# Rotary embedding on half the head: from sixteen 2 MB tiles to four 8 MB tiles, with tables broadcast over heads

## Chip, core and metric

The kernel runs on one core of a Trainium2 chip. The metric is the time of one execution on the device in microseconds (us), the median of several runs. Traces come from one profiled execution.

## What is computed

x has the shape (16, 512, 16, 64): batch, sequence, heads, dim, in fp32. That is 33.55 MB, read once and written once. Of each head's 64 numbers the first 32 are rotated in pairs (element j with element j+16), by a cosine and a sine that depend on the sequence position and on j; the last 32 pass unchanged. Only the first 16 columns of the tables cos and sin, each (512, 32), are used.

```python
x1, x2 = x[..., :32], x[..., 32:]
first  = x1[..., :16] * cos[..., :16] - x1[..., 16:] * sin[..., :16]
second = x1[..., :16] * sin[..., :16] + x1[..., 16:] * cos[..., :16]
return concatenate([first, second, x2], axis=-1)
```

## The kernel before

One tile is one batch element: 512 sequence rows of 1024 numbers, four rows on each of 128 partitions. A tile is 2 MB, and each partition holds one contiguous run of 16 KB of HBM. There are 16 tiles, six buffers for x (pool xp), and four for the products a_t and b_t (pool abp).

The tables come first. POOL issues the loads of cos and sin into cosL and sinL (L39, L40), on the software queue q0. POOL then spreads them over the heads and over the two halves of a rotated block, into CCX and SSX, one copy for each of the four rows (L49, L50). So CCX and SSX have an element for every element that VectorE multiplies.

Then a loop runs over the 16 tiles. SP issues the load of x_t (L57). VectorE (DVE in the profile) multiplies the first half of each head by the cosines into a_t (L64) and by the sines into b_t (L65), and writes differences and sums of quarters back into x_t (L66, L72). ACT issues the store of the whole tile, with the untouched half in it (L79). The in-place result means that an x buffer is free only when its store has landed; SP's seventh load waits for the first store. Loads run on the queue q1 or q10, stores on the other; both feed the same 16 DMA engines. The order within each engine's instructions is set by the framework's scheduler from the dependences, and semaphores connect the engines.

Of the kernel before, what the change touches and what calls it, by code (L numbers as in the profile page):

```python
# [1 line left out]

# [4 lines left out]


@with_exitstack  # L10
def kernel(
    ctx: ExitStack,
    tc: tile.TileContext,
    x: bass.AP,
    cos: bass.AP,
    sin: bass.AP,
    out: bass.AP,
):
    nc = tc.nc
    fp32 = mybir.dt.float32  # L20

    B, S, H, D = x.shape
    Q = D // 4
    HF = D // 2
    P = 128
    K = S // P

    xf = x.rearrange("b (p k) h d -> b p (k h d)", p=P)
    of = out.rearrange("b (p k) h d -> b p (k h d)", p=P)
    cosf = cos.rearrange("(p k) j -> p (k j)", p=P)  # L30
    sinf = sin.rearrange("(p k) j -> p (k j)", p=P)

    const_pool = ctx.enter_context(tc.tile_pool(name="const", bufs=1))
    x_pool = ctx.enter_context(tc.tile_pool(name="xp", bufs=6))
    ab_pool = ctx.enter_context(tc.tile_pool(name="abp", bufs=4))

    cosL = const_pool.tile([P, K, HF], fp32)
    sinL = const_pool.tile([P, K, HF], fp32)
    nc.gpsimd.dma_start(out=cosL[:], in_=cosf)  # L39
    nc.gpsimd.dma_start(out=sinL[:], in_=sinf)  # L40

    CCX = const_pool.tile([P, K, H, 2, Q], fp32)
    SSX = const_pool.tile([P, K, H, 2, Q], fp32)
    for k in range(K):
        dst_c = CCX[:, k].rearrange("p h c j -> p (h c) j")
        dst_s = SSX[:, k].rearrange("p h c j -> p (h c) j")
        src_c = cosL[:, k : k + 1, 0:Q].to_broadcast((P, 2 * H, Q))
        src_s = sinL[:, k : k + 1, 0:Q].to_broadcast((P, 2 * H, Q))
        nc.gpsimd.tensor_copy(out=dst_c, in_=src_c)  # L49
        nc.gpsimd.tensor_copy(out=dst_s, in_=src_s)  # L50

    cc_op = CCX.rearrange("p k h c j -> p (k h) (c j)")
    ss_op = SSX.rearrange("p k h c j -> p (k h) (c j)")

    for b in range(B):
        x_t = x_pool.tile([P, K, H, D], fp32)
        nc.sync.dma_start(out=x_t.rearrange("p k h d -> p (k h d)"), in_=xf[b])  # L57

        a_t = ab_pool.tile([P, K * H, HF], fp32)
        b_t = ab_pool.tile([P, K * H, HF], fp32)  # L60

        x12 = x_t.rearrange("p k h d -> p (k h) d")[:, :, 0:HF]

        nc.vector.tensor_mul(out=a_t[:], in0=x12, in1=cc_op)  # L64
        nc.vector.tensor_mul(out=b_t[:], in0=x12, in1=ss_op)  # L65
        nc.vector.tensor_tensor(  # L66
            out=x12[:, :, 0:Q],
            in0=a_t[:, :, 0:Q],
            in1=b_t[:, :, Q : 2 * Q],
            op=mybir.AluOpType.subtract,  # L70
        )
        nc.vector.tensor_tensor(  # L72
            out=x12[:, :, Q : 2 * Q],
            in0=a_t[:, :, Q : 2 * Q],
            in1=b_t[:, :, 0:Q],
            op=mybir.AluOpType.add,
        )

        nc.scalar.dma_start(out=of[b], in_=x_t.rearrange("p k h d -> p (k h d)"))  # L79


# [1 line left out]
_INS = ['x', 'cos', 'sin']  # L83
_OUTS = [((16, 512, 16, 64), 'float32')]


# [23 lines left out]
```

## Time and profile before

| | before |
|---|---|
| median of 9 runs | 163.16 us (162.98 to 163.54) |
| the profiled execution | 163.15 us |
| its span in the trace | 161.4 us |
| VectorE busy | 108.7 us |
| GpSimd (POOL) busy | 6.0 us |
| moved by DMA | 67.25 MB, mean 417 GB/s over the span |
| first store issued | 19.2 us |

The span runs from the first to the last record of the program; what the execution's time has beyond it is start and end that the trace does not show. Issuing a transfer is not counted as busy time. "DMA" in the rows by time is the mean busy share of the 16 DMA engines.

### The profile page before, as it was taken

What the parts mean: (1) busy time and instruction counts of PE and PEld (TensorE: products, weight loads), DVE (VectorE), ACT (ScalarE), POOL (GpSimd) and SP (SyncE); (2) the same over time, 40 slices, a digit from 0 to 9 for tenths busy, and PEclk for the clock granted to TensorE, in tenths of its full rate; (3) what the DMA queues carried; (4) which work ended last, traced back from release to release, by engine and by line L of the source; (5) the groups of instructions that cost most, each with busy time, mean ns of one, the idle gap of its engine ahead of it and who ended that gap; (6) DMA issues with size and microseconds to landing.
All of it is one profiled execution on the core that took longest, in us unless ns stands there. A gap on an engine that the chain in (4) does not pass through costs nothing.

```text
span 161.4 us, 189 instructions
## 1 busy us (share of the span) xinstructions
DVE 108.7 (67%) x64; POOL 6.0 (4%) x14
## 2 busy tenths in 40 slices
DVE  0009999999995692948849296592947939389300
POOL 3190000000000000000000000000000000000000
DMA  5999999999999999999999999999999999999994
GB/s 158 426 430 430 418 386 426 443 422 435 439 422 430 439 414 443 422 430 447 414 439 439 422 435 430 430 430 422 439 439 418 439 435 424 430 426 439 435 414 207
DMA packets 4673, 67.25 MB, mean 417 GB/s; under 512 B 544, under 2 KB 544, under 8 KB 576
## 3 DMA queue, kind: packets, MB, share of 16 engines
q1 hardware_dynamic: 2304, 33.56, 49.4%
q10 hardware_dynamic: 2304, 33.56, 48.6%
q0 software_dynamic: 64, 0.13, 0.2%
q14 instruction: 1, 0.01, 0.0%
HBM read 33.69 MB, written 33.55 MB: 417 GB/s over the span
## 4 chain that ended last, share of the span: by engine, by line
DMA 60%; DVE 28%; POOL 2%; issue 2%; DVEq 1%; POOLq 0%; SPq 0%; PEldq 0%
DMA out_dram<-x_t 32%; DMA x_t<-in_x_dram 24%; DVE a_t L64 9%; DVE b_t L65 8%; DVE x_t L66 6%; DVE x_t L72 5%; DMA cosL<-in_cos_dram 4%; POOL CCX L49 1%; DVEq L105 1%; POOL SSX L50 1%; POOLq L105 0%; SPq L57 0%; DVEq L66 0%; PEldq L105 0%
## 5 line engine op out<-in xcount | busy, mean ns | idle before, releaser
L64 DVE TENSOR_TENSOR a_t<-x_t,CCX 128x2048 f32<-128x2048 f32 x16 | 37.0, 2314 | 41.9 <-DMA x_t<-in_x_dram 30.0
L65 DVE TENSOR_TENSOR b_t<-x_t,SSX 128x2048 f32<-128x2048 f32 x16 | 36.6, 2285 | 0.0
L66 DVE TENSOR_TENSOR x_t<-a_t,b_t 128x1024 f32<-128x1024 f32 x16 | 19.6, 1222 | 0.2
L72 DVE TENSOR_TENSOR x_t<-a_t,b_t 128x1024 f32<-128x1024 f32 x16 | 19.5, 1219 | 0.0
L49 POOL COPY CCX<-cosL 128x512 f32<-128x512 f32 x4 | 2.4, 615 | 5.1 <-DMA cosL<-in_cos_dram 5.1
L50 POOL COPY SSX<-sinL 128x512 f32<-128x512 f32 x4 | 2.4, 616 | 0.3 <-DMA sinL<-in_sin_dram 0.3
L39 POOL DMA_DIRECT2D cosL<-in_cos_dram x1 | 0.7, 671 | 0.8 <-PEq L105 0.8
L40 POOL DMA_DIRECT2D sinL<-in_sin_dram x1 | 0.5, 537 | 0.0
L94 POOL MEMSET const-float32-0.0<- 128x1 f32 x1 | 0.1, 100 | 0.2 <-issue 0.2
L94 POOL MEMSET const-bfloat16-1.0<- 128x1 bf16 x1 | 0.1, 103 | 0.0
L94 POOL MEMSET const-uint8-127<- 128x1 uint8 x1 | 0.1, 103 | 0.0
L94 POOL MEMSET const-float32-1.0<- 128x1 f32 x1 | 0.1, 100 | 0.0
## 6 DMA issues: line engine op xcount, KB each, us to landing
x_t<-in_x_dram SPq DMA_DIRECT2D x16, 2048.0 KB, 19.4
out_dram<-x_t ACTq DMA_DIRECT2D x16, 2048.0 KB, 24.1
cosL<-in_cos_dram POOLq DMA_DIRECT2D x1, 64.0 KB, 6.3
sinL<-in_sin_dram POOLq DMA_DIRECT2D x1, 64.0 KB, 7.1
```

The lines of the kernel that those rows point to most:

```text
L39: nc.gpsimd.dma_start(out=cosL[:], in_=cosf)
L40: nc.gpsimd.dma_start(out=sinL[:], in_=sinf)
L49: nc.gpsimd.tensor_copy(out=dst_c, in_=src_c)
L50: nc.gpsimd.tensor_copy(out=dst_s, in_=src_s)
L64: nc.vector.tensor_mul(out=a_t[:], in0=x12, in1=cc_op)
L65: nc.vector.tensor_mul(out=b_t[:], in0=x12, in1=ss_op)
L66: nc.vector.tensor_tensor(out=x12[:, :, 0:Q], in0=a_t[:, :, 0:Q], in1=b_t[:, :, Q : 2 * Q], op=mybir.AluOpType.subtract,)
L72: nc.vector.tensor_tensor(out=x12[:, :, Q : 2 * Q], in0=a_t[:, :, Q : 2 * Q], in1=b_t[:, :, 0:Q], op=mybir.AluOpType.add,)
L94: nc = _bacc.Bacc("TRN2", target_bir_lowering=False, num_devices=1)
L105: with _tile.TileContext(nc) as tc:
```

## The change

The sequence rows are cut differently: 16 rows to a partition (K = 16), so a tile is four batch elements, 8 MB, and a partition holds one contiguous run of 64 KB. There are four tiles and three buffers for x. SP loads the first tile in pieces of 4, 4 and 8 rows per partition, the second and third whole, and the fourth in two halves. Three tiles are stored whole and the fourth in halves.

With 16 rows on a partition, 32 partitions hold all 512 positions, and the table repeats every 32 partitions. ACT loads cos and sin into 32 partitions (stage), and four copies, two by VectorE and two by POOL, write the used columns twice over into each group of 32 partitions of table. CCX and SSX are gone: VectorE reads the table with a step of zero over the heads.

VectorE works in chunks of four rows per partition (KC = 4), the same 128x4096 elements as a tile before. The sine products go into b_t, which now lies in PSUM, with two buffers; the cosine products are written in place into x_t, so a_t is gone.

```diff
-    K = S // P
-    x_pool = ctx.enter_context(tc.tile_pool(name="xp", bufs=6))
-    ab_pool = ctx.enter_context(tc.tile_pool(name="abp", bufs=4))
-    nc.gpsimd.dma_start(out=cosL[:], in_=cosf)
-    nc.gpsimd.dma_start(out=sinL[:], in_=sinf)
...
+    K = 16
+    T = B * S // (P * K)
+    PB = S // K
+    REP = P // PB
+    xf = x.rearrange("b s h d -> (b s h d)").rearrange("(t p f) -> t p f", t=T, p=P)
...
+    x_pool = ctx.enter_context(tc.tile_pool(name="xp", bufs=3))
+    b_pool = ctx.enter_context(tc.tile_pool(name="bp", bufs=2, space=bass.MemoryType.PSUM))
+    stage = const_pool.tile([PB, 2, K, HF], fp32)
+    nc.scalar.dma_start(out=stage[:, 0].rearrange("p k j -> p (k j)"), in_=cosf)
+    nc.scalar.dma_start(out=stage[:, 1].rearrange("p k j -> p (k j)"), in_=sinf)
+    table = const_pool.tile([P, 2, K, 2, Q], fp32)
+    for r in range(REP):
+        eng = nc.vector if r % 2 == 0 else nc.gpsimd
+        eng.tensor_copy(
+            out=table[r * PB : (r + 1) * PB].rearrange("p t k c j -> p (t k) c j"),
+            in_=stage.rearrange("p t k j -> p (t k) j")[:, :, 0:Q]
+            .unsqueeze(2)
+            .to_broadcast((PB, 2 * K, 2, Q)),
+        )
...
+    KC = 4
+    loads = [[4, 4, 8]] + [[16]] * (T - 2) + [[8, 8]]
+    stores = [[16]] * (T - 1) + [[8, 8]]
     for t in range(T):
         x_t = x_pool.tile([P, K, H, D], fp32)
+        for n in loads[t]:
+            nc.sync.dma_start(
+                out=x_f[:, k0 * R : (k0 + n) * R], in_=xf[t, :, k0 * R : (k0 + n) * R]
+            )
...
+        for k0 in range(0, K, KC):
+            x1 = x_t[:, k0 : k0 + KC, :, 0:HF]
+            c = C[:, k0 : k0 + KC].unsqueeze(2).to_broadcast((P, KC, H, HF))
+            s = Sn[:, k0 : k0 + KC].unsqueeze(2).to_broadcast((P, KC, H, HF))
+            b_t = b_pool.tile([P, KC, H, HF], fp32)
+            nc.vector.tensor_mul(out=b_t[:], in0=x1, in1=s)
+            nc.vector.tensor_mul(out=x1, in0=x1, in1=c)
+            nc.vector.tensor_sub(
+                out=x1[:, :, :, 0:Q], in0=x1[:, :, :, 0:Q], in1=b_t[:, :, :, Q:HF]
+            )
+            nc.vector.tensor_add(
+                out=x1[:, :, :, Q:HF], in0=x1[:, :, :, Q:HF], in1=b_t[:, :, :, 0:Q]
+            )
+            for lo, hi in ends:
+                if hi == k0 + KC:
+                    nc.scalar.dma_start(
+                        out=of[t, :, lo * R : hi * R], in_=x_f[:, lo * R : hi * R]
+                    )
```

In the changed kernel the table copies are L50, the loads of x L68, the four VectorE operations L81, L82, L83 and L86, and the stores L91. The scheduler keeps the order chunk by chunk for the first two chunks and then interleaves the chunks in pairs.

More of the change, by code (lines that the diff above doesn't have):

```diff
@@ L20 @@
     fp32 = mybir.dt.float32
+    P = 128
     B, S, H, D = x.shape
@@ L24 @@
     HF = D // 2
-    P = 128
-    K = S // P
[L28 to L31, printed above, removed]
-    const_pool = ctx.enter_context(tc.tile_pool(name="const", bufs=1))
-    x_pool = ctx.enter_context(tc.tile_pool(name="xp", bufs=6))
-    ab_pool = ctx.enter_context(tc.tile_pool(name="abp", bufs=4))
-    cosL = const_pool.tile([P, K, HF], fp32)
@@ L38 @@
-    sinL = const_pool.tile([P, K, HF], fp32)
-    nc.gpsimd.dma_start(out=cosL[:], in_=cosf)
-    nc.gpsimd.dma_start(out=sinL[:], in_=sinf)
[L42 to L50, printed above, removed]
@@ L52 @@
-    cc_op = CCX.rearrange("p k h c j -> p (k h) (c j)")
-    ss_op = SSX.rearrange("p k h c j -> p (k h) (c j)")
-    for b in range(B):
-        x_t = x_pool.tile([P, K, H, D], fp32)
[L57 to L79, printed above, removed]
+    K = 16
@@ new lines @@
+    T = B * S // (P * K)
+    PB = S // K
+    REP = P // PB
+    R = H * D
+    xf = x.rearrange("b s h d -> (b s h d)").rearrange("(t p f) -> t p f", t=T, p=P)
+    of = out.rearrange("b s h d -> (b s h d)").rearrange("(t p f) -> t p f", t=T, p=P)
+    cosf = cos.rearrange("(p k) j -> p (k j)", k=K)
+    sinf = sin.rearrange("(p k) j -> p (k j)", k=K)
+    const_pool = ctx.enter_context(tc.tile_pool(name="const", bufs=1))
+    x_pool = ctx.enter_context(tc.tile_pool(name="xp", bufs=3))
+    b_pool = ctx.enter_context(tc.tile_pool(name="bp", bufs=2, space=bass.MemoryType.PSUM))
@@ new lines @@
+    C = table[:, 0].rearrange("p k c j -> p k (c j)")
+    Sn = table[:, 1].rearrange("p k c j -> p k (c j)")
+    KC = 4
+    loads = [[4, 4, 8]] + [[16]] * (T - 2) + [[8, 8]]
+    stores = [[16]] * (T - 1) + [[8, 8]]
+    for t in range(T):
+        x_t = x_pool.tile([P, K, H, D], fp32)
+        x_f = x_t.rearrange("p k h d -> p (k h d)")
+        k0 = 0
+        for n in loads[t]:
+            nc.sync.dma_start(
+                out=x_f[:, k0 * R : (k0 + n) * R], in_=xf[t, :, k0 * R : (k0 + n) * R]
+            )
+            k0 += n
+        ends, k0 = [], 0
+        for n in stores[t]:
+            ends.append((k0, k0 + n))
+            k0 += n
+        for k0 in range(0, K, KC):
[16 more added lines that the diff above has]
+                    )
```

## Prediction

> **What bounds the kernel now.** I read the page's second and third parts first, because a kernel that loads everything, does four VectorE operations and stores everything can be bound by either side.
>
> ```profile
> span 161.4 us, 189 instructions
> DVE 108.7 (67%) x64; POOL 6.0 (4%) x14
> DMA  5999999999999999999999999999999999999994
> DMA packets 4673, 67.25 MB, mean 417 GB/s; under 512 B 544, under 2 KB 544, under 8 KB 576
> q1 hardware_dynamic: 2304, 33.56, 49.4%
> q10 hardware_dynamic: 2304, 33.56, 48.6%
> DMA 60%; DVE 28%; POOL 2%; issue 2%; DVEq 1%; POOLq 0%; SPq 0%; PEldq 0%
> L64 DVE TENSOR_TENSOR a_t<-x_t,CCX 128x2048 f32<-128x2048 f32 x16 | 37.0, 2314 | 41.9 <-DMA x_t<-in_x_dram 30.0
> ```
>
> The DMA row is full from the second slice to the last but one, while DVE is busy for 67%. The chain gives DVE 28%, but those steps lie where the DMA row shows a 9 as well: the chain follows one order of release and does not say that the DMA engines rested. The wait of 30.0 us at L64 is DVE waiting for data. So the question is where the 16 DMA engines do not run at full rate. Then the table by windows (columns: window, length, DVE busy, POOL busy, clock, DMA share, GB/s):
>
> ```profile
> 0.00:4.00 4.00, 0.00 (x0) 1.41 (x6) 1.00 0.56 152
> 4.00:20.00 16.00, 8.07 (x5) 4.57 (x8) 1.00 1.01 430
> 20.00:24.00 4.00, 3.96 (x3) 0.00 (x0) 1.00 0.97 369
> 24.00:158.00 134.00, 96.67 (x58) 0.00 (x0) 1.00 1.01 431
> 158.00:161.40 3.40, 0.00 (x0) 0.00 (x0) 1.00 0.36 154
> ```
>
> At 431 GB/s the 67.25 MB need 156.0 us. The first 4 us move 0.61 MB, worth 1.4 us: 2.6 lost. The window 20 to 24, where the first store (issued at 19.2) begins, loses 4 x (431-369)/431 = 0.6. The last 3.4 us move 0.52 MB: 2.2 lost, mostly after the last byte. 156.0+2.6+0.6+2.2 = 161.4, the span. The profiled execution took 163.15, so 1.75 us lie around the span; the median of the 9 runs is 163.16, the same within 0.01.
>
> [...]with equal rows q1 and q10 move 33.56 MB each, and loads (19.4 us to landing) and stores (24.1) each stay about two transfers deep at one transfer per 9.7 us. [...]The trace shows only a pitch of 16 KB, at 431/2 = 215.5 per direction. [...]no PSUM operation is in the trace.
>
> **The change part by part.**
>
> *Transfers.* 16 loads and 16 stores of 2 MB become 7 loads and 5 stores of 2, 4 or 8 MB, with the same x bytes, and two table loads stay. Rows per engine go from 256 of 16 KB to 96: loads 24+8+8+16, stores 8+8+8+16. One 16 KB row takes 16 x 16384/431000 = 0.608 us of an engine[...]. [...] I take -0.6.
>
> *Start.* SP still issues a 2 MB load first (0.75 us); the table loads move from POOL to ACT, which had nothing to issue until 19.2. Same bytes: 0, between -0.3 and +0.3. POOL loses its two issues (0.67+0.54 us), which nobody else waits behind.
>
> *Tables.* Eight POOL copies of 512 (4.8 us) become two on DVE and two on POOL of 1024 elements. With a POOL copy at 0.615 us for 512, one of 1024 is 1.2[...]. In pairs side by side 2.4 us, one after another at most 4.8. The cos load took 6.3 us to land; from ACT at about 0.8 that gives 7.1 (bounds 3 and 8), so tables are ready at about 9.5 (5 to 13). Before, DVE began at 11.9. The first 2 MB are moved by 2.6+4.9 = 7.5, seen at about 9.5. Covered entirely: the first store is later than this by four chunks and DMA has three tiles to load meanwhile.
>
> *VectorE.* Work per 128x4096 elements stays 2048+2048+1024+1024. Before, one set takes 6.80 us from start to start (19.07 to 25.87). b_t in PSUM is touched by three of four operations[...]; the extra order waits on DVE's own results cost about 0.1 us (2.32 against 2.21 us from start to start in the row of L65). A broadcast table (step 0 over heads) is not in the trace: 0 to +0.2, taken 0[...]. I take 7.05 us per chunk, 6.8 to 7.3. Hidden by the DMA if stores never run dry, which is the next step.
>
> *Order of work, at 431 and equal shares.* The load pieces of tile 0 are seen at 9.5, 14.3 and 24.1. Chunks 0 and 1 end by 23.6, chunks 2 and 3 at 38.2; store 0 (8.39 MB) moves from 39.5. Until then loads ran alone and have moved 15.9 MB. Tile 1 needs 0.9 MB more at half rate: 43.4, seen at 45.4; DVE idles 7 us, then works to 73.6, store 1 is queued by 75. Store 0 ends at 39.5+38.9 = 78.4. SP's load of tile 3 waits for it, with nothing behind it on SP but that tile's second half; tile 2's load still runs (43.4+38.9 = 82.3), so the load queue never empties. Tile 2 is computed from 84.4 to 112.6, store 2 queued at 114. Tile 3's halves arrive at 101.8 and 121.3 (+2). Store 1 ends at 117.3. Store 2 has half rate until 121.3, then all: 138.8. Last halves of the compute end at 126.7 and 140.8; their stores are queued by 128 and 142 behind store 2, and run to 148.6 and 158.3. The last one is in the queue 6.6 us before its turn. So each queue that stops leaves the other one full, and the later first store (39 against 19) costs no DMA time. If an engine serves whole rows in turn, tile 3's 32 KB rows get a third beside 64 KB stores: the second half arrives near 130, the last store is queued near 147.5, 1 us ahead of its turn. Still 0, but the cover is thin.
>
> *Store start.* The 0.6 us hole should recur near 39 us: 0, between -0.6 and +1 with longer rows. Reads alone last 20 us longer, at 430 against 431: +0.05.
>
> **Sum**: 161.4-0.6+0.05 = 160.8, plus 1.75: about 162.5 us.
>
> **Rivals.**
> 1. *The pitch in HBM slows every transfer.* Neighbouring partitions lie 64 KB apart instead of 16 in all stages. [...] Against: [...]every tile is one contiguous 8 MB. It decides from a loss of 0.2%, or 0.6% if the row saving comes in full.[...]
> 2. *Rows bring nothing*, because bytes set the 431 or because a 64 KB row is cut into packets as short as today's, so that the change is not what it says: 163.2 us. For it: the DMA share is 1.00 already.
> 3. *VectorE becomes the bound at the end.* DVE has two idle stretches (7 and 11 us) while whole 8 MB loads land. If stores take two thirds throughout and a chunk takes 7.5 us, tile 3's second half is ready some 4 us after store 2 and its first half have drained: about 166.5. Even split and 7.05 us speak against; at even shares it takes 8.5 us a chunk.
>
> **How the numbers follow.** A measurement of this kernel tells about 0.2%, 0.33 us, from no change. Longer rows at work: 0.50, all faster. Rival 2: 0.22, no change. Slower: rival 1 0.18, rival 3 and a larger hole at the store's start 0.10. [...]High end: rival 1 with its estimate, 165.3, which leaves out about one in ten above. If DMA goes as I say, 161.6 to 163.3 is its own range.
>
> **What would show it.** Right: far fewer packets on q1 and q10; a rate of 433 to 434 in the windows of both directions; a full DMA row; L81 near 2.3 us; idle of DVE before tiles 1 and 2; the last store issued near 142. Wrong: a rate under 430 in steady windows (rival 1), packets of 16 KB or a rate of 431 (rival 2), a gap in the DMA row after 120 us (rival 3), a deeper slice near 39 us.

## The result and the profile after

The changed kernel takes 181.65 us (median of 10 runs, 180.3 to 183.23) where the kernel before takes 163.17 (31 runs). The ratio is 1.1114, with a 95% interval of 1.1095 to 1.1134: 11% slower. The forecast was 162.5 us with a range of 161.0 to 165.3. The profiled execution took 183.64 us, with a span of 181.9; it is some 2 us longer than the median, so a loss read from its trace can be too large by as much.

The page after, in the lines that answer to those shown of before:

```profile
span 181.9 us, 145 instructions
DVE 109.6 (60%) x66; POOL 3.2 (2%) x6
DMA  6999979999899989798999999999999989400595
DMA packets 1825, 67.25 MB, mean 370 GB/s; under 512 B 224, under 2 KB 224, under 8 KB 288
q1 hardware_dynamic: 1008, 33.55, 46.0%
q10 hardware_dynamic: 816, 33.69, 44.5%
...
L81 DVE TENSOR_TENSOR b_t<-x_t,table 128x2048 f32<-128x2048 f32 x16 | 36.1, 2296 | 51.6 <-DMA x_t<-in_x_dram 50.6
```

Same bytes, fewer packets, nearly the same VectorE work (109.6 us, before 108.7). The DMA row, however, has a hole near its end (4, 0, 0), and the wait for data at the first operation of a chunk has grown from 30.0 to 50.6 us. The windows say where the 16 DMA engines lost time (columns as before: window, length, DVE busy, POOL busy, clock, DMA share, GB/s):

```profile
44.00:92.00 48.00, 25.80 (x16) 0.00 (x0) 1.00 0.99 378
92.00:120.00 28.00, 26.76 (x16) 0.00 (x0) 1.00 0.97 396
120.00:155.00 35.00, 13.42 (x8) 0.00 (x0) 1.00 1.00 426
155.00:170.00 15.00, 13.42 (x8) 0.00 (x0) 1.00 0.15 63
```

Against 431 GB/s the first window loses 48 x 53/431 = 5.9 us, the second 2.3, the third 0.4 and the last 12.8: 21.4 us, where the spans differ by 20.5. So there are two losses: a **low rate** with loads and stores together, some 8 us, and a **gap** before the last store, some 13. The DMA share of 0.99 in the first window hides the first loss: packets are in flight, but each takes longer (a 64 KB row of a load 3.0 us, where undisturbed ones below take 2.42).

The gap is seen in the timeline of VectorE and of the queue of stores (start, duration, engine and line, names; in brackets the idle time before and its cause):

```profile
38.83 131.33 ACTq L91 DMA_DIRECT2D out_dram<-x_t  x5
92.37 4.50 DVE L81 TENSOR_TENSOR b_t<-x_t,table 128x2048 f32<-128x2048 f32 x2 [22.57 <-DMA x_t<-in_x_dram]
123.28 4.50 DVE L81 TENSOR_TENSOR b_t<-x_t,table 128x2048 f32<-128x2048 f32 x2 [4.15 <-DMA x_t<-in_x_dram]
156.37 4.50 DVE L81 TENSOR_TENSOR b_t<-x_t,table 128x2048 f32<-128x2048 f32 x2 [19.67 <-DMA x_t<-in_x_dram]
```

The third tile is seen at 92.4 us and the halves of the fourth at 123.3 and 156.4; the prediction had 84.4, 103.8 and 123.3. After 156.4 VectorE needs 13.4 us for the last two chunks. The other stores have drained in that time (the last piece lands at 165.6), and the last store is issued at 169.8, with its last piece landed at 180.6. A transfer leaves 16 landing records in the trace, as many as there are DMA engines, and I read them as one for each engine. Those of the last half tile lie between 133.0 and 155.9 us, with a median of 140.3: VectorE waits for the slowest of the 16.

### The profile page after: what moved, and what is told of

It is laid out like the page before. It is cut to its first block, busy times and chain, and to the rows that moved or that the text cites. A ratio compares the mean times of both kernels' runs of the same rounds, so it can differ in the third digit from the quotient of the medians.

```text
span 181.9 us, 145 instructions
## 1 busy us (share of the span) xinstructions
DVE 109.6 (60%) x66; POOL 3.2 (2%) x6
## 4 chain that ended last, share of the span: by engine, by line
another core or an unknown queue 49%; DMA 29%; DVE 13%; issue 1%; DVEq 1%; SPq 0%
DMA x_t<-in_x_dram 29%; DVE x_t L82 5%; DVE b_t L81 4%; DVE x_t L83 2%; DVE x_t L86 2%; DVEq L119 1%; SPq L68 0%; DVEq L81 0%
## 5 line engine op out<-in xcount | busy, mean ns | idle before, releaser
L81 DVE TENSOR_TENSOR b_t<-x_t,table 128x2048 f32<-128x2048 f32 x16 | 36.1, 2296 | 51.6 <-DMA x_t<-in_x_dram 50.6
L82 DVE TENSOR_TENSOR x_t<-x_t,table 128x2048 f32<-128x2048 f32 x16 | 36.0, 2286 | 0.1
L83 DVE TENSOR_TENSOR x_t<-x_t,b_t 128x1024 f32<-128x1024 f32 x16 | 19.5, 1216 | 0.1
L86 DVE TENSOR_TENSOR x_t<-x_t,b_t 128x1024 f32<-128x1024 f32 x16 | 19.5, 1216 | 0.0
L50 DVE COPY table<-stage 32x1024 f32<-32x1024 f32 x2 | 2.1, 1055 | 8.5 <-DMA stage<-in_sin_dram 8.5
L50 POOL COPY table<-stage 32x1024 f32<-32x1024 f32 x2 | 3.0, 1475 | 8.1 <-DMA stage<-in_sin_dram 8.1
```

The costliest lines, as they stand in the source:

```text
L50: eng.tensor_copy(out=table[r * PB : (r + 1) * PB].rearrange("p t k c j -> p (t k) c j"), in_=stage.rearrange("p t k j -> p (t k) j")[:, : ...
L81: nc.vector.tensor_mul(out=b_t[:], in0=x1, in1=s)
L82: nc.vector.tensor_mul(out=x1, in0=x1, in1=c)
L83: nc.vector.tensor_sub(out=x1[:, :, :, 0:Q], in0=x1[:, :, :, 0:Q], in1=b_t[:, :, :, Q:HF])
L86: nc.vector.tensor_add(out=x1[:, :, :, Q:HF], in0=x1[:, :, :, Q:HF], in1=b_t[:, :, :, 0:Q])
```

## The experiments

Theory A: a DMA engine serves a whole row of one queue and then a whole row of the other, so 32 KB loads beside 64 KB stores get a third of the rate; and 64 KB rows on both queues lose rate. Theory B: the 64 KB pitch in HBM slows loads and stores together. Theory C: whole 8 MB tiles in three buffers starve VectorE, whatever the rows.

**Short rows at the same pitch.**

```diff
-    loads = [[4, 4, 8]] + [[16]] * (T - 2) + [[8, 8]]
-    stores = [[16]] * (T - 1) + [[8, 8]]
+    loads = [[4, 4, 4, 4]] * T
+    stores = [[4, 4, 4, 4]] * T
```

> The changed kernel with every load and store cut into pieces of 4 sequence rows: 16 KB runs per partition, but the same 8 MB tiles, three buffers and the same 64 KB pitch in HBM. Theory A (long rows: an engine serves whole rows in turn, and two queues of 64 KB rows lose rate): steady windows with loads and stores back at 428 to 431 GB/s, the last store in its queue before its turn, 162.5 to 164.5 us. Theory B (the 64 KB pitch in HBM slows loads and stores together): mixed windows stay near 385 GB/s, so 67.25 MB take over 170 us; 172 to 178 us. Theory C (whole 8 MB tiles and three buffers starve VectorE, whatever the rows): the release of the first buffer still waits for the whole first tile's stores; a gap in the DMA row before the last store remains, 172 us or more.

Measured: 163.51 us, ratio 1.0017 (1.0010 to 1.0023). Its windows:

```profile
44.00:92.00 48.00, 33.78 (x20) 0.00 (x0) 1.00 1.01 431
92.00:158.00 66.00, 42.89 (x26) 0.00 (x0) 1.00 1.01 431
```

The full rate is back at the same pitch, and so is the time, with 8 MB tiles, three buffers, PSUM and the broadcast table as in the changed kernel. B falls, and so does C as far as it blames tiles and buffers whatever the transfers: the whole loss hangs on how the transfers are cut. The pieces also let VectorE start before a whole tile is there, and the stores at 18.1 us instead of 38.8, so this edit doesn't separate the rows from that.

**Shares by rows.** Two edits make the rows of the fourth tile's loads and the stores beside them equal, once at 32 KB and once at 64 KB.

```diff
-    stores = [[16]] * (T - 1) + [[8, 8]]
+    stores = [[16]] + [[8, 8]] * (T - 1)
```

> Only the stores of the second and third tile are cut in halves (32 KB rows), so that they meet the fourth tile's 32 KB loads with equal rows. Theory A (whole rows in turn): the fourth tile's loads get half the rate instead of about 0.3 of it; its second half lands near 136 instead of 156 us, the DMA gap before the last store closes for the most part, 167 to 172 us. Theory B (pitch) and C (tile size): the loads' share does not depend on the stores' rows; within 2 us of the changed kernel's 181.7.

```diff
-    loads = [[4, 4, 8]] + [[16]] * (T - 2) + [[8, 8]]
+    loads = [[4, 4, 8]] + [[16]] * (T - 1)
```

> Only the fourth tile is loaded whole (64 KB rows) instead of in halves, so its rows are as long as the stores'. Theory A: it lands near 136 to 140 us as a whole, VectorE needs 27 us for its four chunks, the last half store (10 us) ends near 176 to 180: 177 to 182 us, with the landing at least 15 us earlier than the second half's 156 us. Theory C, and any theory in which rows do not set the shares: it lands at 156 us as the second half did, and VectorE begins all four chunks only then: 190 us or more.

Measured: 172.85 us (ratio 1.0588, 1.0507 to 1.0669) and 177.26 (1.0858, 1.0800 to 1.0916). The start of VectorE on what came last, from the timelines of the two kernels:

```profile
138.39 4.50 DVE L81 TENSOR_TENSOR b_t<-x_t,table 128x2048 f32<-128x2048 f32 x2 [6.19 <-DMA x_t<-in_x_dram]
```

```profile
137.37 4.50 DVE L81 TENSOR_TENSOR b_t<-x_t,table 128x2048 f32<-128x2048 f32 x2 [19.43 <-DMA x_t<-in_x_dram]
```

With equal rows the second half, or the whole tile, is there 18 or 19 us sooner than at 156.4, although no load was moved ahead in the first edit and the load was made coarser in the second. Part of this is the lag between the 16 landings. In the changed kernel it grows from 6.5 us for the third tile to 22.9 for the last half. With the halved stores it shrinks from 9.2 to 5.8, and the median landing of the last half comes at 135.3 instead of 140.3. Both times lie where theory A put them (the first by 0.85 us above its bound). The low rate between 44 and 92 us stays in both:

```profile
44.00:92.00 48.00, 26.76 (x16) 0.00 (x0) 1.00 0.98 393
```

```profile
44.00:92.00 48.00, 27.58 (x17) 0.00 (x0) 1.00 1.00 378
```

**All rows 32 KB, and half-size tiles.** In the first kernel every load after the first 4 MB and every store has 32 KB rows, with 8 MB tiles and three buffers. The second has eight sequence rows per partition, 4 MB tiles and six buffers.

```diff
-    loads = [[4, 4, 8]] + [[16]] * (T - 2) + [[8, 8]]
-    stores = [[16]] * (T - 1) + [[8, 8]]
+    loads = [[4, 4, 8]] + [[8, 8]] * (T - 1)
+    stores = [[8, 8]] * T
```

> The changed kernel with 32 KB rows in every load and store after the first 4 MB (8 MB tiles, three buffers and 64 KB pitch as they are). Equal rows: even shares and no gap at the end; if 32 KB rows don't lose rate here, as in the kernel with eight rows per partition, 162.5 to 164 us. A theory in which the 8 MB tiles and three buffers starve VectorE whatever the rows: over 168 us.

```diff
-    K = 16
+    K = 8
...
-    x_pool = ctx.enter_context(tc.tile_pool(name="xp", bufs=3))
+    x_pool = ctx.enter_context(tc.tile_pool(name="xp", bufs=6))
...
-    loads = [[4, 4, 8]] + [[16]] * (T - 2) + [[8, 8]]
-    stores = [[16]] * (T - 1) + [[8, 8]]
+    loads = [[4, 4]] + [[8]] * (T - 1)
+    stores = [[8]] * T
```

> Eight sequence rows per partition: 4 MB tiles, rows and pitch of 32 KB, six buffers (the same memory), first tile loaded in halves, every other transfer whole. Theory A: all rows of loads and stores are equal after the first tile, so shares are even; whatever 32 KB rows lose in rate lies between none (16 KB) and 11% (64 KB): mixed windows 405 to 430 GB/s, 163 to 168 us. Theory B: the same range, from the pitch. Theory C: half the tile halves the waits, six buffers instead of three; 163 to 165 us.

Measured: 163.29 us, ratio 1.0001 (0.9988 to 1.0014), and 162.61 us, ratio 0.9963 (0.9948 to 0.9977). C is answered a second time by the first. The second, with 4 MB tiles, is 0.4% faster than the kernel before, and below every range that I had given for it. Windows of the kernel before, then of this one:

```profile
4.00:24.00 20.00, 12.03 (x7) 4.57 (x8) 1.00 1.00 418
44.00:152.00 108.00, 76.77 (x46) 0.00 (x0) 1.00 1.01 431
```

```profile
4.00:24.00 20.00, 11.27 (x7) 0.85 (x1) 1.00 1.02 425
24.00:158.00 134.00, 96.73 (x59) 0.00 (x0) 1.00 1.01 433
44.00:152.00 108.00, 76.77 (x47) 0.00 (x0) 1.00 1.00 432
```

Part of the difference lies in the first 24 us, where the kernel before already has stores (from 19.2 us; here the first is issued at 27.0) and has its dip. The other part is the steady rate. A window is a coarse measure of it (one row of 32 KB on 16 engines is 0.5 MB), but the packet records of the trace are not: a 16 KB row takes 611 ns in the kernel before, and a 32 KB row 1213 in this one, 9 less than two short ones. Between 24 and 158 us, 433 GB/s against the 431 of the kernel before are worth 0.6 us.

**Transfers alone.** A kernel with no arithmetic and no tables separates the queues from everything else:

```python
for k0 in range(0, K, 4):      # SP: first tile, 16 KB rows
    nc.sync.dma_start(out=a_f[:, k0 * R : (k0 + 4) * R], in_=xf[0, :, k0 * R : (k0 + 4) * R])
for t in range(1, T):          # SP: the others, rows of NL x 4 KB
    for k0 in range(0, K, NL): ...
for t in range(T):             # ACT: the first tile, to all places, rows of NS x 4 KB
    for k0 in range(0, K, NS): ...
```

(NL, NS) is (16, 16), (4, 16), (4, 4) and (8, 8).

> Transfers alone, all arithmetic and the tables left out: SP loads the first 8 MB tile in four pieces and then the three others whole (64 KB rows); as soon as the first tile is there, ACT stores that same tile four times, to all four places of the output, whole (64 KB rows). Nothing waits for VectorE, so both queues are full from about 21 us until the loads end. Theory A1 (two queues of 64 KB rows lose rate by themselves): 370 to 400 GB/s in every window with both, span over 168 us. Theory A2 (the loss between 44 and 92 us came from when and where those transfers met, since loads of the fourth tile beside stores ran at 427 later): 425 to 431 nearly throughout, span 160 to 163 us.

> The same transfers alone (arithmetic and tables left out), loads in pieces with 16 KB rows, stores whole with 64 KB rows. Whole rows in turn: loads get one fifth of the rate (85 GB/s or less) while stores run, so the stores end near 120 us and about 17 MB of loads come after them, near 160 us. Shares by bytes, independent of the rows: loads get half and end near 140 us, the stores after them.

> The same transfers alone (arithmetic and tables left out), loads and stores both in pieces with 16 KB rows at the 64 KB pitch. Any theory of the rows: 430 GB/s throughout, span 160 to 161.5 us; a theory of the pitch: below 420 in the windows with both.

> The same transfers alone (arithmetic and tables left out), loads and stores both with 32 KB rows. A1: between the 64 KB and the 16 KB case; as the kernel with eight rows per partition showed no loss with rows of 32 KB, I expect 425 to 432 GB/s and a span of 160 to 162 us.

Measured, one run each: 161.51, 165.74, 162.44 and 162.08 us, spans 159.7, 164.0, 160.7 and 160.3. The 64 KB case:

```profile
4.00:20.00 16.00, 0.00 (x0) 1.00 1.00 429
44.00:150.00 106.00, 0.00 (x0) 1.00 1.01 435
```

So two queues of 64 KB rows lose nothing by themselves: A1, half of my theory, fell. The second kernel gives the shares. In the trace's packet records, between 44 and 60 us loads move 84 GB/s and stores 349, between 60 and 75 us 86 and 347: loads get 0.19 and 0.20 of the sum, for rows of 16 against 64 KB. That is near the 16/(16+64) = 0.20 of one row for one row. Its span missed my number (164 against 160). ACT issued the third store only at 77 us and the fourth at 113, so the store queue was empty for two stretches; the shares are read before the first.

The records also give the price of a row where nothing disturbs it: 611 ns for 16 KB, 1213 for 32, 2418 for 64. That is 602 ns for every 16 KB and about 9 for every row, so longer rows do gain a little (1213 ns against 2 x 611, 2418 against 4 x 611). Counted from the records between 44 and 140 us, the traces with 16 KB rows run at 431 GB/s, those with 32 KB at 432 to 433, and those with 64 KB and the first store at 22.6 or 32.0 us at 433 and 434.

**When the first store comes.** Additions on the last quarter of the first tile hold back its store; rotation and tables are left out as above.

```diff
+    for i in range(8):          # 7 and 4 in the others
+        a1 = a_t[:, 12:16, :, 0:HF]
+        nc.vector.tensor_add(out=a1, in0=a1, in1=a1)
```

> The transfers alone with 64 KB rows as in m1_64_64 (the rotation and the tables left out), but the first store waits for eight VectorE additions on the first tile (18 us), so it starts near 40 us, as in the changed kernel, when the second tile's load is seven eighths done, and not near 21 us when it begins. If the loss of the changed kernel between 44 and 92 us comes from where the first store meets the loads: 375 to 400 GB/s after 44 us for some tens of us, rows longer than 2.42 us, span 163 us or more. If it comes from the rest of the kernel (VectorE work during transfers, releases): 425 to 431, span 160 to 161 us.

> As m5_64_64_late with four additions (rotation and tables left out), so that the first store starts near 31 us, in the middle of the second tile's load. If the moment of the meeting decides: a loss between m1_64_64 (none) and m5_64_64_late, or either; the row durations tell. If m5_64_64_late has no loss, neither has this.

> As m5_64_64_late (rotation and tables left out, first store near 40 us), with rows of 32 KB on both sides. If the loss needs a late first store and 64 KB rows: 425 to 432 GB/s, span 160 to 162 us. If a late first store is enough: the same loss as in m5_64_64_late.

> The transfers alone with 64 KB rows as in m5_64_64_late (rotation and tables left out), with seven additions instead of eight, so that the first store is issued at 38.9 us as in the changed kernel. If the moment of the first store decides: load rows of 3 us and more until about 100 us, landings of one transfer spread by 5 us or more over the 16 engines, span 165 us or more. If not: as m5_64_64_late or better, span 160 to 162.5 us.

Measured, one run each: 163.92 us with the first store issued at 41.2, 161.81 at 32.0, and 180.91 at 38.9. The first lies between its two forecasts: a small loss, not 375 to 400 GB/s. The 32 KB kernel (161.97) missed its purpose: only its second half store waits for the additions, the first went out at 12.9 us. Windows of the kernel with the store at 41.2, then of that at 38.9:

```profile
44.00:92.00 48.00, 0.00 (x0) 0.00 (x0) 1.00 0.96 415
92.00:158.00 66.00, 0.00 (x0) 0.00 (x0) 1.00 0.99 428
```

```profile
44.00:92.00 48.00, 0.00 (x0) 0.00 (x0) 1.00 0.99 370
44.00:140.00 96.00, 0.00 (x0) 0.00 (x0) 1.00 0.97 362
```

The last kernel is idle on every compute engine after 39 us, is the same as the first of these four but for one addition, and loses 19.4 us of span against the store at 22.6 (179.1 against 159.7). In its packet records a 64 KB load takes 3.1 us and a store 2.8 between 92 and 120 us, instead of 2.42 each, and one transfer's 16 landings lie 4.8 to 6.1 us apart, where they lay 0.5 to 0.6 apart with the early store.

**The tables, and the moment in the changed kernel.** Three runs ask what puts the engines out of step: the small table rows, or the moment alone. The first adds the table loads to the transfers alone, the other two hold back the first store of the changed kernel.

```diff
+    stage = a_pool.tile([PB, 2, K, HF], fp32)
+    nc.scalar.dma_start(out=stage[:, 0].rearrange("p k j -> p (k j)"), in_=cosf)
+    nc.scalar.dma_start(out=stage[:, 1].rearrange("p k j -> p (k j)"), in_=sinf)
```

> As n1_64_64_39 with the two table loads on ACT's queue at the start (the rotation and the use of the tables left out). If the small table rows put the 16 engines out of step, and engines out of step slow each other with 64 KB rows: span over 165 us here and not in n1_64_64_39. If the tables do nothing: within 1 us of n1_64_64_39.

```diff
-            nc.vector.tensor_mul(out=b_t[:], in0=x1, in1=s)
+            for _ in range(5 if t == 0 and k0 == 12 else 1):      # 2 in the other
+                nc.vector.tensor_mul(out=b_t[:], in0=x1, in1=s)
```

> The changed kernel with one operation of L81 done twice for the last chunk of the first tile (its result is the same), so that the first store is issued 2.2 us later, near 41 us. If the moment of the first store sets the loss: 375 to 395 GB/s between 44 and 92 us becomes another rate, and the time moves by several us (170 to 180 us). If it does not matter: 181 to 184 us.

> The same with that operation done five times: first store near 48 us, after the second tile has landed. If the loss starts where the first store meets the end of the second tile's load: no loss, at least 415 GB/s from 50 to 92 us; the last half tile still comes late because of its shorter rows, 170 to 178 us. If not: the loss stays and the time is 182 to 190 us.

Measured: 181.82 us with the tables (one run, first store at 39.7 us; 180.91 without): they are not needed for the loss. The changed kernel with its first store at 41.0 us takes 180.25 (ratio 1.1047, 1.0879 to 1.1216), and with the first store at 47.7 us, after 9 us of extra VectorE work, 171.05 (two runs, 169.33 and 172.77, no interval). Windows of the latter, whose trace is that of the run of 172.77:

```profile
44.00:92.00 48.00, 47.62 (x29) 0.00 (x0) 1.00 1.02 436
92.00:145.00 53.00, 22.87 (x15) 0.00 (x0) 1.00 0.99 425
145.00:160.00 15.00, 13.42 (x8) 0.00 (x0) 1.00 0.34 146
```

```profile
74.68 4.50 DVE L82 TENSOR_TENSOR b_t<-x_t,table 128x2048 f32<-128x2048 f32 x2 [0.34 <-DMA x_t<-in_x_dram]
145.50 4.50 DVE L82 TENSOR_TENSOR b_t<-x_t,table 128x2048 f32<-128x2048 f32 x2 [15.44 <-DMA x_t<-in_x_dram]
```

(L82 is the operation of L81, one line lower in this kernel.) A later first store makes the kernel some 10 us faster: the low rate is gone (436 against 378). What is left is the gap, some 10 us between 145 and 160. The third tile is there at 74.7, earlier than forecast, but the fourth tile's 32 KB rows get only 0.32 to 0.35 of the rate beside 64 KB stores, and the last half comes at 145.5; an even share from 85.7 on, where those rows begin, would bring it near 125, an estimate. So the shares by rows make a gap without the low rate. With the store at 41.0 the rate between 44 and 92 us is 416, but the last half comes at 151.8 (its landings lie 26 us apart) and the gap stays, so the time hardly moves and misses its forecast of 170 to 180 by a little.

## Why the prediction was wrong

**What bounds the kernel**: right. The rate of the DMA engines, 431 GB/s and with longer rows up to 434, was the floor, and no kernel here went below 161.5 us.

**Transfers, -0.6 us**: an estimate of mine that no trace of before showed; right in kind, but hidden here by the losses. By the records a row costs about 9 ns (611, 1213, 2418 ns). The 602 ns per 16 KB that remain are 16 x 16384 / 602 = 435 GB/s, an estimate, from these times, of the rate if a row cost nothing. Of the changed kernel itself no window shows the gain; the kernel with 4 MB tiles and 32 KB rows does.

**Start and tables**: right in kind. The tables landed by about 8.5 us, the copies took 1.06 us on DVE and 1.48 on POOL, and the first chunk began at 11.5 (taken: 9.5, bound 13), hidden as said.

**VectorE**: hidden, as said, until the gap opened, and PSUM cost next to nothing. L81 takes 2296 ns with its output in PSUM, before 2285; L83 and L86, which read PSUM, take 1216, before 1222 and 1219. Two chunks in a pair take 13.3 us against my 14.1, a little under my range; the 7.05 us that I took for a chunk held an estimate for PSUM that no trace of before showed.

**Order of work, "at 431 and equal shares"**: this step failed, in both of its words. The halved stores and the (4, 16) transfers show that rows decide the shares (16 KB loads beside 64 KB stores got 0.19 and 0.20); in the changed kernel the fourth tile's loads got 0.34 of the rate between 98 and 110 us. I had the row-by-row case in the text, from the same even traffic that could not tell it from shares by bytes, and costed it at 0, with the second half near 130 us and 1 us of cover. That 130 leaned on two things that I did not write down. One is a stretch without stores: redone with a third for the loads, store 1 ends at 108.6 and store 2 is queued at 114, and in between the loads have the engines to themselves. The other is that all 16 engines keep step. With the low rate the third tile came at 92.4 and not at 84.4, and the fourth tile's load was issued at 92.5, where I had it moving from 82.3. The last of store 1's 16 pieces landed at 121.3, when store 2 had been issued (119.2), so the slowest engine had no such stretch. If a 64 KB store row stands before each of an engine's 16 load rows, they take 16 x (1.21 + 2.42) = 58 us; from about 98 us that gives 156, an estimate from the row times, and the last piece landed at 155.9.

**Store start, "-0.6 to +1"**: mis-sized. It was not a hole of 1 us at most but a loss of rate for 75 us (378 GB/s between 44 and 92 us, 396 from there to 120), some 8 us in all, set by the moment of the first store (38.8 us; with it at 47.7, 436 between 44 and 92 us).

**Rivals**: 1, the pitch, is refuted by the 16 KB rows at 431; its price, and with it the high end of 165.3, was an estimate of mine that no trace showed, and so was the low end of 161.0. 2, that rows bring nothing, is refuted by the row times: the packets are as long as the rows (records of 16384, 32768 and 65536 bytes), and a long one costs a little less for its bytes (2418 ns against 4 x 611). 3, VectorE at the end, is what happened, by the wait that I named (the second half of the fourth tile), but at 13 us and not 4, and with a tenth of the chance. Only one of its two conditions was met: the stores did take two thirds, but a chunk took 6.7 us and not 7.5. In place of the other stood a late fourth tile and engines out of step, which I did not price.

**What stays open**: why 64 KB rows put the engines out of step and slow them when the first store is issued between 38.6 and 39.7 us (five traces, 365 to 393 GB/s between 44 and 92 us), with a much smaller loss of rate at 41.0 and 41.2 (416 and 415), and none at 22.6, 32.0 and 47.7. The kernels with transfers alone ran once each. Rows of 16 and 32 KB never showed it here, but their first stores were issued by 27 us, so the row length is not shown to be a condition.

## What to carry to other kernels

Where two queues share the DMA engines, cut loads and stores into rows of the same length: here the queue with the shorter rows got the smaller share (0.19 and 0.20 for 16 KB beside 64, 0.32 to 0.35 for 32 beside 64, 0.50 with 16 on both in the kernel before between 44 and 140 us), and its last half tile came late (156.4 us; 138.4 with rows of 32 KB on both). Rows of 32 KB instead of 16 bought half a percent of rate here with the engines full (433 GB/s against 431 between 24 and 158 us); 8 MB tiles left three buffers where 4 MB tiles had six, and with 32 KB rows took 163.29 us against 162.61. Estimate a last landing for the slowest DMA engine: here it came 15.6 us after the median one, and a cover of 1 us was no cover.

## What the runs showed of the hardware that I had not expected

A load queue of 16 KB rows beside a store queue of 64 KB rows gets a fifth of the rate (0.19 and 0.20; 84 and 86 GB/s beside 349 and 347). An undisturbed row costs about 9 ns beside 602 for each 16 KB (611, 1213 and 2418 ns for 16, 32 and 64 KB). With transfers alone, issuing the first store 2.4 us earlier (one addition less ahead of it) changed the span from 162.1 to 179.1 us, one run each, and a DMA share of 0.97 to 1.00 stood beside 362 to 378 GB/s, where kernels without the loss show 1.01 beside 431 to 435: the share counts packets in flight, not work done. VectorE paid nothing that could be seen for PSUM operands in fp32 (written, L81, 2296 ns, before 2285; read, L83 and L86, 1216, before 1222 and 1219), nor for a table read with a step of zero (L82: 2286 ns, L64 before: 2314).
